# The first two column jobs of the in projection and of FFN up as plain products

## The chip, the cores and the metric

The kernel runs on one core of one Trainium2 chip. The time is device microseconds of one launch, and what is compared is the median of several runs. Engines are named as in the profile: PE is TensorE (matmuls and transposes), DVE VectorE, ACT ScalarE, POOL GpSimd, SP SyncE, which here only issues DMAs.

## The reference

One decoder layer, 1024 time steps of width 1024, float32 throughout:

```python
h = rmsnorm(x, norm_mix)
proj = h @ w_in                     # 1024 x N_IN; q, k, v, gates of three mixers
x = x + merged(gla, mlstm, fox) @ w_out
h = rmsnorm(x, norm_ffn)
u = causal_dwconv(h @ w_up, conv_w, conv_b)
a, g = jnp.split(u, 2, axis=-1)
x = x + (silu(g) * a) @ w_down
return rmsnorm(x, norm_final)
```

The two products that matter here are `h @ w_in`, and `h @ w_up` with its 5632 columns.

## The kernel before, in words

**Numbers.** A float32 product is made of three float32r matmuls: each operand is split into hi (a cast by ACT) and lo (source minus hi, by DVE) in `split` (L254), and the products hi x hi, hi x lo and lo x hi are added in PSUM (`prod`, L1135). One product of 512 by 512 by 512 is so 12 matmuls of 128x512. Operands live transposed: the moving side is a tile x of 128 features by 512 time steps.

**Jobs.** A `Job` (L45) makes two column tiles (m = 0, 1) of 128 columns over both time halves (hf = 0, 1) and both halves of the 1024 features (kh). That is eight block products; it needs seven, in the Winograd form of Strassen's scheme. They are numbered in the order 1, 5, 6, 2, 7, 3, 4. Each has a combination of the four weight blocks (`prep`, L1160, sums by POOL, then `wsplit`) and a combination of the four blocks of h. Call these b (the first half's eight blocks b0 to b7) and the second half's. x1 and x2 are blocks of the first time half; x3 is a block of the second; x5, x6, x7 and x4 are sums over both halves. The moving combinations are the same for all jobs of a stage. They are made once, put into the tiles g0 to g6 of the pool `big` (`put`, L344; `MAP_IN` and `MAP_FF` tell which) and stay for the whole stage.

**A stage's start.** The first four rows of 128 time steps are loaded, normalised and transposed (`blocks0`, L331), which gives x1 and x2; the second four follow (`blocks1`, L352), which makes x5, x6, x3, x7 and x4. `products` (L146) begins with the first two jobs, LEADS = 2, the leads: `rounds` (L182) takes them product by product, 1 for both, 2 for both, then 5, 6, 3, 7 and 4, so that work with x1 and x2 covers the making of the sums. From the third job on ("job 2", counted from 0) jobs run one after the other. `gemms` (L1233) prepares weights AHEAD = 2 products before they are used. In the in projection (`start`, L383) the leads are the gqk jobs of heads 0 and 1, job 2 is the first mx job. In the FFN the leads are the first two up jobs; their u tiles go through the convolution on DVE (L1316).

**Output.** The `post` functions (L1259, L1270) take a finished product out of PSUM: with a second operand by a DVE addition, without by an ACT copy; those of the in projection go through tiles st to DRAM by DMAs on SP. Near the end of the leads SP also loads wif and bt (L456, L464) for the small products pa<-wif,bt of the mLSTM gates, which PE computes between those of job 2.

**Order.** Each engine works off its own queue in order. The framework's scheduler places instructions of the whole program in those queues by its own estimates, so a change in the stage's start also shifts what stands next to what in the mixers. In the FFN's last stretch the finished activations come back as the down operand xd, whose splits use the tiles of `big` as they become free.

Of the kernel before, what the change touches and what calls it, by code (L numbers as in the profile page):

```python
# [35 lines left out]
MAP_IN = {1: 0, 2: 1, 5: 2, 6: 3, 3: 4, 7: 5, 4: 6}  # L36
MAP_FF = {1: 1, 2: 2, 5: 3, 6: 4, 3: 0, 7: 5, 4: 6}
# [4 lines left out]
KEEP = 14  # L42


class Job:  # L45
# [3 lines left out]
    def __init__(self, src1, src2, xc, post, name, nk=4, done=None, wide=False, kept=None):  # L49
        self.src, self.xc, self.post, self.name, self.nk = (src1, src2), xc, post, name, nk  # L50
        self.done, self.wide, self.kept = done, wide, kept
        self.raw, self.w, self.after = None, {}, {}
# [93 lines left out]
def products(jobs, lead=0, tail=0):  # L146


    yield from rounds(jobs[:lead])
# [24 lines left out]
def ending(jobs):  # L174

    yield from rounds(jobs, ROUND[:4])
    for j in jobs:
        for p in (7, 3, 4):
            yield j, p

# [8 lines left out]
class Kern:  # L189
# [162 lines left out]
    def blocks1(self, xs, b, pool, gain, xc, base, qtile, ttile):  # L352
        nc = self.nc
        t1, b22 = [], []
        for i in range(4):
            ps = self.turn4(xs, i)
            t = ttile(i)
            nc.vector.scalar_tensor_tensor(out=t, in0=ps, scalar=self.col(gain, i), in1=b[i],
                                           op0=ALU.mult, op1=ALU.subtract)
            t1.append(t)  # L360
            self.put(xc, 5, i, t, base)
        yield
        for i in range(4):
            ps = self.turn4(xs, 4 + i)
            q = qtile(i)
            nc.scalar.activation(q, ps, AF.Copy, scale=self.col(gain, 4 + i))
            b22.append(q)
            nc.vector.tensor_tensor(out=t1[i], in0=q, in1=t1[i], op=ALU.subtract)  # L368
            self.put(xc, 6, i, t1[i], base)
        yield  # L370
        for i in range(4):
            self.put(xc, 3, i, b22[i], base)
# [10 lines left out]
    def start(self, pool, xc, stream):  # L383
# [12 lines left out]
        xs = [self.norm(x, pool, i % 2) for i, x in enumerate(xs)]  # L396
        b = self.blocks0(xs, pool, "nm")
        xs = [load(tt) for tt in range(4, 8)]
        for i in range(4):
            self.put(xc, 1, i, b[i], MAP_IN)  # L400
        next(stream)
        next(stream)
        xs = [self.norm(x, pool, i % 2) for i, x in enumerate(xs)]
        for i in range(4):
            self.put(xc, 2, i, b[4 + i], MAP_IN, self.nc.gpsimd if i < 2 else None)
        for _ in range(2):
            next(stream)
        for _ in self.blocks1(xs, b, pool, "nm", xc, MAP_IN,
                                           lambda i: pool.tile([P, 512], F32, tag=f"q{i}", name=f"b22_{i}"),
                                           lambda i: pool.tile([P, 512], F32, tag="xs", name="t1", bufs=4)):  # L410
            for _ in range(2):
# [761 lines left out]

# [604 lines left out]
```

## Time and profile before

| | |
|---|---|
| runs | 2437.90, 2440.86, 2442.22 us; median 2440.86 us |
| profiled execution | 2440.24 us, span of its instructions 2438.4 us |
| PE | 2360.6 us busy, 97% of the span |
| DVE | 1599.3 us, 66% |
| ACT | 1145.9 us, 47% |
| POOL | 676.7 us, 28% |
| DMA | mean 130 GB/s |

The table's busy times are for the whole span. A stretch of the program is read from the busy time by stretch and from each engine's instructions in order of time. The lead stages are short: in the in projection from 20 us, in the FFN from 1748 us, each some 60 us.

### The profile page before, as it was taken

What the parts mean: (1) busy time and instruction counts of PE and PEld (TensorE: products, weight loads), DVE (VectorE), ACT (ScalarE), POOL (GpSimd) and SP (SyncE); (2) the same over time, 40 slices, a digit from 0 to 9 for tenths busy, and PEclk for the clock granted to TensorE, in tenths of its full rate; (3) what the DMA queues carried; (4) which work ended last, traced back from release to release, by engine and by line L of the source; (5) the groups of instructions that cost most, each with busy time, mean ns of one, the idle gap of its engine ahead of it and who ended that gap; (6) DMA issues with size and microseconds to landing.
All of it is one profiled execution on the core that took longest, in us unless ns stands there. A gap on an engine that the chain in (4) does not pass through costs nothing.

```text
span 2438.4 us, 32792 instructions
## 1 busy us (share of the span) xinstructions
PE 2360.6 (97%) x11359; PEld 1949.6 (80%) x11359; DVE 1599.3 (66%) x2871; ACT 1145.9 (47%) x2268; POOL 676.7 (28%) x752
## 2 busy tenths in 40 slices
PE   6999999989999999999999999999989999999998
PEld 4887778878888888888888888888868888888886
DVE  7697556767677775877776624534588998986223
ACT  5345455555566664555554512213355555554112
POOL 5222234444354443222222100000244443420000
PEclk9999999999999999999999999999999999999999
DMA  3355444545434444343343735421122222228232
GB/s 136 104 171 177 137 133 155 167 156 180 153 121 141 144 147 147 121 139 131 123 132 106 261 111 171 163 96 61 69 83 90 78 87 78 80 81 275 90 100 92
DMA packets 158500, 316.33 MB, mean 130 GB/s; under 512 B 16456, under 2 KB 56168, under 8 KB 157824
## 3 DMA queue, kind: packets, MB, share of 16 engines
q1 hardware_dynamic: 158336, 314.26, 39.0%
q8 instruction: 89, 1.46, 0.2%
q14 instruction: 75, 0.61, 0.1%
HBM read 218.61 MB, written 95.58 MB: 129 GB/s over the span
## 4 chain that ended last, share of the span: by engine, by line
PE 79%; DVE 8%; DMA 4%; ACT 3%; POOL 3%; issue 2%; SPq 0%; DVEq 0%; POOLq 0%; ACTq 0%
PE pg L248 49%; PE pa L248 28%; PE pa L252 3%; DMA mw<-mw_d 1%; DVE x L256 1%; POOL sum L1171 1%; POOL sm L261 1%; DVE w3l L256 0%; DVE st L1279 0%; DMA fv<-fv_d 0%; DMA fvo_raw<-in_w_in 0%; POOL mw L634 0%; DVE t L368 0%; DVE c L1316 0%; DVE e L805 0%
## 5 line engine op out<-in xcount | busy, mean ns | idle before, releaser
L248 PE MATMUL pg<-x,w6h 128*128 128x512 f32 x560 | 182.6, 404 | 11.8 <-DVE x L256 10.6
L248 PE MATMUL pg<-x,w4h 128*128 128x512 f32 x560 | 175.5, 394 | 1.3 <-DVE xm L1267 0.8
L248 PE MATMUL pg<-x,w1h 128*128 128x512 f32 x560 | 176.4, 395 | 0.0
L248 PE MATMUL pg<-x,w7h 128*128 128x512 f32 x560 | 175.2, 393 | 0.7 <-ACT u L1202 0.7
L248 PE MATMUL pg<-x,woh 128*128 128x512 f32 x512 | 158.1, 390 | 0.0
L248 PE MATMUL pa<-x,woh 128*128 128x512 f32 x512 | 157.7, 389 | 0.0
L1171 POOL TENSOR_TENSOR sum<-up_raw 128x512 f32<-128x512 f32 x44 | 87.5, 1989 | 227.1 <-DMA up_raw<-in_w_up 175.6
L1316 DVE SCALAR_TENSOR_TENSOR c<-u,cols,c 128x1022 f32<-128x1022 f32 x84 | 128.1, 1525 | 15.8 <-ACT c L1312 15.6
L248 PEld LDWEIGHTS pg<-x,w6h 128*128 128x128 f32 x560 | 106.1, 193 | 38.1 <-DVE x L256 14.1
L261 POOL TENSOR_TENSOR sm<-sm,mhalf 128x1 f32<-128x1 f32 (+1 forms) x32 | 27.9, 874 | 381.4 <-DVE sm L260 381.3
L248 PE MATMUL pg<-x,w2h 128*128 128x512 f32 x384 | 123.4, 398 | 1.6 <-POOL x L256 1.5
L248 PE MATMUL pg<-x,w5h 128*128 128x512 f32 x384 | 122.8, 398 | 0.9 <-DVE x L256 0.6
L248 PEld LDWEIGHTS pg<-x,w4h 128*128 128x128 f32 x560 | 103.7, 188 | 24.2 <-DVE xm L1267 1.2
L248 PE MATMUL pg<-x,w3h 128*128 128x512 f32 x384 | 123.0, 399 | 0.0
L248 PEld LDWEIGHTS pg<-x,w1h 128*128 128x128 f32 x560 | 103.8, 189 | 21.1 <-DVE x L256 0.5
L248 PEld LDWEIGHTS pg<-x,w7h 128*128 128x128 f32 x560 | 102.9, 188 | 22.0 <-ACT u L1202 1.2
L255 ACT CAST woh<-br_raw 128x512 fp32r<-128x512 f32 x48 | 29.9, 622 | 184.1 <-PE pa L248 177.4
L248 PE MATMUL pg<-x,w6l 128*128 128x512 f32 x280 | 112.9, 403 | 0.0
L248 PEld LDWEIGHTS pa<-x,woh 128*128 128x128 f32 x512 | 96.1, 188 | 20.0
L248 PEld LDWEIGHTS pg<-x,woh 128*128 128x128 f32 x512 | 96.1, 188 | 19.8
L248 PE MATMUL pg<-x,w1l 128*128 128x512 f32 x280 | 109.7, 392 | 0.0
L248 PE MATMUL pg<-x,w7l 128*128 128x512 f32 x280 | 109.4, 391 | 0.0
(459 smaller groups left out, 6748.1 us busy)
## 6 DMA issues: line engine op xcount, KB each, us to landing
up_raw<-in_w_up SPq DMA_DIRECT2D x44, 512.0 KB, 3.9
dn_raw<-in_w_dn SPq DMA_DIRECT2D x30, 512.0 KB, 4.0
gate_raw<-in_w_in SPq DMA_DIRECT2D x24, 512.0 KB, 3.7
g_d<-st SPq DMA_DIRECT2D x48, 256.0 KB, 2.4
yb<-y_d SPq DMA_DIRECT2D x48, 256.0 KB, 4.0
br_raw<-in_w_br SPq DMA_DIRECT2D x24, 512.0 KB, 4.6
gth<-g_d SPq DMA_DIRECT2D x48, 256.0 KB, 2.6
f_d<-c SPq DMA_DIRECT2D x22, 512.0 KB, 2.9
```

What stands on the lines that cost most here:

```text
L248: self.nc.tensor.matmul(out, lhsT=lhsT, rhs=rhs, start=start, stop=stop, skip_group_check=skip)
L252: self.nc.tensor.transpose(out=out, in_=in_, identity=self.ident[:k, :k])
L255: self.nc.scalar.copy(out=hi, in_=src)
L256: (eng or self.nc.vector).tensor_tensor(out=lo, in0=src, in1=hi.bitcast(F32), op=ALU.subtract)
L261: nc.gpsimd.tensor_tensor(out=out, in0=tmp, in1=self.mhalf[:, :n], op=ALU.pow)
L1171: self.nc.gpsimd.tensor_tensor(out=t, in0=a, in1=b, op=op)
L1316: nc.vector.scalar_tensor_tensor(out=c[:, s:], in0=u[:, :T - s], scalar=self.col("fw", 44 * tap + m), in1=c[:, s:], op0=ALU.mult, op1=ALU.add)
```

## The change

The leads of both stages are computed as plain products, eight quarters a job in place of seven products: `plain` gives their order, `quarter` computes one. A quarter's key is (hf, kh, m); its weights are a block as it is, without sums on POOL; two quarters add up in one PSUM bank, and ACT copies the result out. First come the eight quarters of the first time half, which need x1 and x2 alone, then eight of the second, which need x3 and a new x8, the other plain block of the second half; x8 lies in g6, where x4 later takes its place. `blocks1` makes x8 and x3 first (by ACT's scaled copy from PSUM), and then, in the program behind the quarters, x5 and x6 (subtractions by DVE) and x7 and x4 (by POOL). In the in projection the second four rows are loaded at once into the tile g5, ahead of the gqk weights, and x2 is split by DVE alone. In the FFN x3 and x7 change tiles, and the down operand takes the tiles in another order (`ROLL_DN`). `n` counts the two leads' products. The core of the diff:

```diff
-MAP_IN = {1: 0, 2: 1, 5: 2, 6: 3, 3: 4, 7: 5, 4: 6}
-MAP_FF = {1: 1, 2: 2, 5: 3, 6: 4, 3: 0, 7: 5, 4: 6}
+MAP_IN = {1: 0, 2: 1, 5: 2, 6: 3, 3: 4, 7: 5, 4: 6, 8: 6}
+MAP_FF = {1: 1, 2: 2, 5: 3, 6: 4, 3: 5, 7: 0, 4: 6, 8: 6}
+ROLL_DN = tuple(MAP_FF[p] for p in (1, 2, 5, 6, 7, 3, 4))
...
 def products(jobs, lead=0, tail=0):
-    yield from rounds(jobs[:lead])
+    yield from plain(jobs[:lead])
...
+def plain(jobs):
+
+    for kh in range(2):
+        for j in jobs:
+            for m in range(2):
+                yield j, (0, kh, m)
+    for j in jobs:
+        for kh in range(2):
+            for m in range(2):
+                yield j, (1, kh, m)
...
     def blocks1(self, xs, b, pool, gain, xc, base, qtile, ttile):
         nc = self.nc
         t1, b22 = [], []
+        for kh, tile, out, p in ((0, ttile, t1, 8), (1, qtile, b22, 3)):
+            for i in range(4):
+                ps = self.turn4(xs, 4 * kh + i)
+                t = tile(i)
+                nc.scalar.activation(t, ps, AF.Copy, scale=self.col(gain, 4 * kh + i))
+                out.append(t)
+                self.put(xc, p, i, t, base)
+            yield
         for i in range(4):
-            ps = self.turn4(xs, i)
-            t = ttile(i)
-            nc.vector.scalar_tensor_tensor(out=t, in0=ps, scalar=self.col(gain, i), in1=b[i],
-                                           op0=ALU.mult, op1=ALU.subtract)
-            t1.append(t)
-            self.put(xc, 5, i, t, base)
+            nc.vector.tensor_tensor(out=t1[i], in0=t1[i], in1=b[i], op=ALU.subtract)
+            self.put(xc, 5, i, t1[i], base)
         yield
         for i in range(4):
-            ps = self.turn4(xs, 4 + i)
-            q = qtile(i)
-            nc.scalar.activation(q, ps, AF.Copy, scale=self.col(gain, 4 + i))
-            b22.append(q)
-            nc.vector.tensor_tensor(out=t1[i], in0=q, in1=t1[i], op=ALU.subtract)
+            nc.vector.tensor_tensor(out=t1[i], in0=b22[i], in1=t1[i], op=ALU.subtract)
             self.put(xc, 6, i, t1[i], base)
-        yield
-        for i in range(4):
-            self.put(xc, 3, i, b22[i], base)
         yield
         for i in range(4):
             nc.gpsimd.tensor_tensor(out=b[i], in0=t1[i], in1=b[i], op=ALU.subtract)
...
         xs = [self.norm(x, pool, i % 2) for i, x in enumerate(xs)]
+        rows = self.group(MAP_IN[7], F32, "x")
+        later = [rows[:, i, :] for i in range(4)]
+        for i in range(4):
+            self.nc.sync.dma_start(out=later[i], in_=self.a["x"][(4 + i) * P:(5 + i) * P, :])
         b = self.blocks0(xs, pool, "nm")
-        xs = [load(tt) for tt in range(4, 8)]
         for i in range(4):
             self.put(xc, 1, i, b[i], MAP_IN)
-        next(stream)
-        next(stream)
-        xs = [self.norm(x, pool, i % 2) for i, x in enumerate(xs)]
+        for _ in range(2 * LEADS):
+            next(stream)
         for i in range(4):
-            self.put(xc, 2, i, b[4 + i], MAP_IN, self.nc.gpsimd if i < 2 else None)
-        for _ in range(2):
+            self.put(xc, 2, i, b[4 + i], MAP_IN)
+        xs = [self.norm(x, pool, i % 2) for i, x in enumerate(later)]
+        for _ in range(2 * LEADS):
             next(stream)
...
+            for _ in range((LEADS, 3 * LEADS)[n] if n < 2 else 0):
                 next(stream)
...
     def prep(self, job, p):
+        if isinstance(p, tuple):
+            _, kh, m = p
+            job.w[p] = self.wsplit(job.raw[2 * m + kh], "wp")
+            return
...
+    def quarter(self, job, hf, kh, m):
+
+        if kh == 0:
+            job.banks[hf, m] = self.pg()
+        bank = job.banks[hf, m]
+        wh, wl = job.w.pop((hf, kh, m))
+        x = job.xc[((1, 2), (8, 3))[hf][kh]]
+        for k in range(4):
+            ks = slice(k * P, (k + 1) * P)
+            xh, xl = x[k]
+            self.mm(bank, wh[:, ks], xh, kh == 0 and k == 0, False, True)
+            self.mm(bank, wh[:, ks], xl, False, False, True)
+            self.mm(bank, wl[:, ks], xh, False, kh == 1 and k == 3, True)
+        if kh:
+            job.post(m, hf, bank, None)
+            if hf and m and job.done is not None:
+                job.done()
...
-            n = 14
+            n = 16
...
-                    g = m // 2 % 7
+                    g = ROLL_DN[m // 2 % 7]
...
-            for _ in range(2 * LEADS):
+            for _ in range(4 * LEADS):
                 next(ff)
...
-                for _ in range(LEADS if n < 3 else 0):
+                for _ in range((LEADS, 3 * LEADS)[n] if n < 2 else 0):
                     next(ff)
```

SP's queue, at the program's start, before: names ending in a number are tiles, gqk_raw the weights of the leads, x_200 to x_206 the second four rows.

```order
L1155 DMA gqk_raw_217<-in_w_in 128x1024
L1155 DMA gqk_raw_219<-in_w_in 128x1024
L1155 DMA gqk_raw_225<-in_w_in 128x1024
L1155 DMA gqk_raw_227<-in_w_in 128x1024
L388 DMA x_200<-in_x 128x1024
L388 DMA x_202<-in_x 128x1024
L388 DMA x_204<-in_x 128x1024
L388 DMA x_206<-in_x 128x1024
```

And now, where x_144 is the tile of the second rows:

```order
L411 DMA x_144<-in_x 128x1024 x4
L1169 DMA gqk_raw_214<-in_w_in 128x1024
L1169 DMA gqk_raw_216<-in_w_in 128x1024
L1169 DMA gqk_raw_226<-in_w_in 128x1024
L1169 DMA gqk_raw_228<-in_w_in 128x1024
L1332 DMA gq_d_105<-st_347 128x512
```

The four row loads have moved from behind the gqk weights to ahead of them.

DVE's queue, in projection, before, where the last moving sums are split: x7 and x4 are tiles of moving sums, w7l and so on the lo parts of weights, st_535 an output tile.

```order
L256 TENSOR_TENSOR x7_560<-b0_149,x7_560 128x512
L256 TENSOR_TENSOR w7l_520<-sum3_517,w7h_519 128x512
L256 TENSOR_TENSOR x7_560<-b1_163,x7_560 128x512
L256 TENSOR_TENSOR w7l_541<-sum3_538,w7h_540 128x512
L1279 TENSOR_TENSOR st_535<-u2_486,pg_391 128x512
L256 TENSOR_TENSOR x7_560<-b2_177,x7_560 128x512
L256 TENSOR_TENSOR x7_560<-b3_191,x7_560 128x512
L256 TENSOR_TENSOR w4l_573<-gqk_raw_219,w4h_572 128x512
L256 TENSOR_TENSOR x4_611<-b4_156,x4_611 128x512
L1279 TENSOR_TENSOR st_556<-u2_506,pg_412 128x512
L256 TENSOR_TENSOR w4l_592<-gqk_raw_227,w4h_591 128x512
L256 TENSOR_TENSOR x4_611<-b5_170,x4_611 128x512
```

And now, from the last subtraction for x6 to the lo part of job 2's sixth weight sum:

```order
L382 TENSOR_TENSOR t1_440<-b22_3_511,t1_440 128x512
L269 TENSOR_TENSOR x7_658<-b0_154,x7_658 128x512
L269 TENSOR_TENSOR x7_658<-b1_168,x7_658 128x512
L269 TENSOR_TENSOR x6_645<-t1_440,x6_645 128x512
L269 TENSOR_TENSOR w5l_613<-sum1_610,w5h_612 128x512
L269 TENSOR_TENSOR x7_658<-b2_182,x7_658 128x512
L269 TENSOR_TENSOR x7_658<-b3_196,x7_658 128x512
L269 TENSOR_TENSOR x4_671<-b4_161,x4_671 128x512
L269 TENSOR_TENSOR x4_671<-b5_175,x4_671 128x512
L269 TENSOR_TENSOR x4_671<-b6_189,x4_671 128x512
L269 TENSOR_TENSOR x4_671<-b7_203,x4_671 128x512
L269 TENSOR_TENSOR w6l_719<-sum2_716,w6h_718 128x512
```

The weight splits and outputs of the leads, which stood between the splits of x7 and x4, are gone from there; w5l and w6l of job 2 stand among and behind these. From x8's first lo part to w6l the queue now has 39 operations.

ACT's queue, in projection, before, around the casts of x4: u2 are copies of a product for later use, st_643 an output tile.

```order
L255 CAST x4_611<-b4_156 128x512
L255 CAST x4_611<-b5_170 128x512
L255 CAST w4h_572<-gqk_raw_219 128x512
L255 CAST x4_611<-b6_184 128x512
L255 CAST x4_611<-b7_198 128x512
L255 CAST w4h_591<-gqk_raw_227 128x512
L255 CAST w1h_627<-mx_raw_623 128x512
L255 CAST w5h_648<-sum1_646 128x512
L255 CAST w6h_702<-sum2_700 128x512
L1283 COPY st_643<-pg_237 128x512
```

And now, where st_607 is the tile whose store stands on SP ahead of the loads of wif and of the first bt:

```order
L268 CAST x7_658<-b2_182 128x512
L268 CAST x6_645<-t1_440 128x512
L268 CAST w5h_612<-sum1_610 128x512
L268 CAST x7_658<-b3_196 128x512
L268 CAST x4_671<-b4_161 128x512
L268 CAST x4_671<-b5_175 128x512
L268 CAST x4_671<-b6_189 128x512
L268 CAST x4_671<-b7_203 128x512
L1322 COPY st_607<-pg_557 128x512
L268 CAST w6h_718<-sum2_716 128x512
```

The copy into st_607 stands behind the last cast of x4, whose source b7 is POOL's eighth subtraction. On PE, pa<-wif,bt moved from ahead of job 2's first product to the inside of its fifth. Near the FFN's end, the splits of the first four down operands now stand on DVE between the last weight splits of FFN up, where before they followed them.

## Rows read from the trace of the kernel before

**Rows 1.** The page: chain by engine, and the group of ACT's casts

```profile
PE 79%; DVE 8%; DMA 4%; ACT 3%; POOL 3%; issue 2%; SPq 0%; DVEq 0%; POOLq 0%; ACTq 0%
...
L255 ACT CAST woh<-br_raw 128x512 fp32r<-128x512 f32 x48 | 29.9, 622 | 184.1 <-PE pa L248 177.4
```

**Rows 2.** Busy time by stretch: length, then busy us of each engine (instructions), granted clock, DMA share

```profile
35.00:63.00 28.00, 19.14 (x81) 13.30 (x80) 27.95 (x25) 15.02 (x29) 21.27 (x13) 0.87 0.17 57
...
1759.00:1795.00 36.00, 25.91 (x102) 19.06 (x100) 29.98 (x33) 18.75 (x35) 21.02 (x13) 0.86 0.10 30
...
2145.00:2189.00 44.00, 44.00 (x195) 36.42 (x194) 35.65 (x40) 23.30 (x35) 10.76 (x7) 1.00 0.14 48
```

**Rows 3.** PE in order of time, in projection: start, us, engine, line, operation, count, [idle, releaser]

```profile
20.03 1.20 PE L248 MATMUL pg<-x,w1h 128*128 128x512 f32 x2
...
34.70 1.91 PE L252 MATMUL pa<-ident,x 128*128 128x128 f32 x16
...
51.09 0.80 PE L248 MATMUL pg<-x,w6h 128*128 128x512 f32 x1 [4.25 <-DVE x L256]
...
69.44 0.62 PE L248 MATMUL pg<-x,w7h 128*128 128x512 f32 x2
...
74.88 0.62 PE L248 MATMUL pg<-x,w4h 128*128 128x512 f32 x2
...
80.32 1.40 PE L248 MATMUL pa<-wif,bt 128*128 128x8 f32 x12
...
89.13 0.48 PE L248 MATMUL pg<-x,w6h 128*128 128x512 f32 x1
...
99.46 0.61 PE L248 MATMUL pg<-x,w1h 128*128 128x512 f32 x2
```

**Rows 4.** PE in order of time, the lead stage of FFN up

```profile
1747.63 0.62 PE L248 MATMUL pg<-x,w1h 128*128 128x512 f32 x2
...
1772.71 1.11 PE L252 MATMUL pa<-ident,x 128*128 128x128 f32 x4 [4.00 <-ACT b L366]
...
1806.72 0.62 PE L248 MATMUL pg<-x,w1h 128*128 128x512 f32 x2
...
1812.16 0.62 PE L248 MATMUL pg<-x,w6h 128*128 128x512 f32 x2
```

**Rows 5.** DVE in order of time, in projection

```profile
36.25 2.06 DVE L358 SCALAR_TENSOR_TENSOR t<-pa,cols,b 128x512 f32<-128x512 f32 x3
...
57.70 0.68 DVE L256 TENSOR_TENSOR w3l<-sum,w3h 128x512 fp32r<-128x512 f32 x1
58.30 1.77 DVE L256 TENSOR_TENSOR x<-b,x 128x512 fp32r<-128x512 f32 x1
60.00 1.75 DVE L256 TENSOR_TENSOR x<-t,x 128x512 fp32r<-128x512 f32 x1
...
78.28 1.82 DVE L256 TENSOR_TENSOR w6l<-sum,w6h 128x512 fp32r<-128x512 f32 x1 [1.59 <-ACT w6h L255]
```

**Rows 6.** DVE in order of time, FFN

```profile
1805.45 0.69 DVE L256 TENSOR_TENSOR w6l<-sum,w6h 128x512 fp32r<-128x512 f32 x1
...
1810.09 1.27 DVE L1316 SCALAR_TENSOR_TENSOR c<-u,cols,c 128x1023 f32<-128x1023 f32 x1
```

**Rows 7.** POOL in order of time, in projection

```profile
33.65 1.30 POOL L1171 TENSOR_TENSOR sum<-sum,gqk_raw 128x512 f32<-128x512 f32 x1 [0.33 <-POOL sm L261]
...
47.10 1.71 POOL L379 TENSOR_TENSOR b<-b,t 128x512 f32<-128x512 f32 x1
```

**Rows 8.** DMA, 0 to 60 us in 40 slices, then issues, 60 to 100 us (KB each, us to landing)

```profile
GB/s 0 205 251 281 369 398 424 407 421 276 38 0 0 35 265 396 371 325 5 0 0 0 5 173 78 109 0 0 0 0 87 268 0 0 0 0 0 60 281 8
...
wif<-in_wif SPq DMA_DIRECT2D x1, 96.0 KB, 4.3
```

**Rows 9.** DVE in order of time, the first splits of the down operand

```profile
2187.07 2.49 DVE L256 TENSOR_TENSOR xd<-dn_raw,xd 128x512 fp32r<-128x512 f32 x4
```

More of the change, by code (lines that the diff above doesn't have):

```diff
@@ L51, in __init__ @@
         self.done, self.wide, self.kept = done, wide, kept
-        self.raw, self.w, self.after = None, {}, {}
+        self.raw, self.w, self.after, self.banks = None, {}, {}, {}
         self.second, self.held, self.inplace, self.sum1 = False, None, False, None
@@ L396, in start @@
         xs = [self.norm(x, pool, i % 2) for i, x in enumerate(xs)]
+        rows = self.group(MAP_IN[7], F32, "x")
+        later = [rows[:, i, :] for i in range(4)]
+        for i in range(4):
+            self.nc.sync.dma_start(out=later[i], in_=self.a["x"][(4 + i) * P:(5 + i) * P, :])
         b = self.blocks0(xs, pool, "nm")
-        xs = [load(tt) for tt in range(4, 8)]
         for i in range(4):
             self.put(xc, 1, i, b[i], MAP_IN)
-        next(stream)
-        next(stream)
-        xs = [self.norm(x, pool, i % 2) for i, x in enumerate(xs)]
+        for _ in range(2 * LEADS):
+            next(stream)
         for i in range(4):
-            self.put(xc, 2, i, b[4 + i], MAP_IN, self.nc.gpsimd if i < 2 else None)
-        for _ in range(2):
+            self.put(xc, 2, i, b[4 + i], MAP_IN)
+        xs = [self.norm(x, pool, i % 2) for i, x in enumerate(later)]
+        for _ in range(2 * LEADS):
             next(stream)
-        for _ in self.blocks1(xs, b, pool, "nm", xc, MAP_IN,
+        for n, _ in enumerate(self.blocks1(xs, b, pool, "nm", xc, MAP_IN,
                                            lambda i: pool.tile([P, 512], F32, tag=f"q{i}", name=f"b22_{i}"),
-                                           lambda i: pool.tile([P, 512], F32, tag="xs", name="t1", bufs=4)):
-            for _ in range(2):
+                                           lambda i: pool.tile([P, 512], F32, tag="xs", name="t1", bufs=4))):
+            for _ in range((LEADS, 3 * LEADS)[n] if n < 2 else 0):
                 next(stream)
@@ L1192, in compute @@
         nc, post = self.nc, job.post
+        if isinstance(p, tuple):
+            self.quarter(job, *p)
+            return
         x = job.xc[p]
@@ L1536, in __call__ @@
             def __call__(self, j, m):
-                if m == 0 and j < LEADS:
-                    return lp.tile([P, T], F32, name=f"ua{j}")
+                if j < LEADS:
+                    return lp.tile([P, T], F32, name=f"u{m}{j}")
                 return self.pool.tile([P, T], F32, tag="u", name="u", bufs=4)
@@ L1620, in body @@
                 pass
-            for _ in range(2 * LEADS):
+            for _ in range(4 * LEADS):
                 next(ff)
             for n, _ in enumerate(k.blocks1([rows[tt] for tt in range(4, 8)], b, hp, "nf", xc, MAP_FF,
-                               lambda i: hp.tile([P, 512], F32, tag=f"q{i}", name="b22"),
+                               lambda i: hp.tile([P, 512], F32, name="b22") if i == 3 else
+                               k.swp.tile([P, 512], F32, tag="ws", name="b22", bufs=3),
                                lambda i: env["wide"].tile([P, 512], F32, tag="S", name="t1", bufs=4))):
-                for _ in range(LEADS if n < 3 else 0):
+                for _ in range((LEADS, 3 * LEADS)[n] if n < 2 else 0):
                     next(ff)
```

## Prediction

> **What bounds the kernel now.** The page's fifth section and its chain of waits come first: in the chain that ended last TensorE (PE) has 79% and VectorE (DVE) 8% [rows 1]. So time is won only where PE stands still or runs at its lower clock. The busy time by stretch says where that is: in 35 to 63 us PE works 19.14 of 28 us at a granted clock of 0.87, and in 1759 to 1795 us 25.91 of 36 us at 0.86; DVE is then busy for 27.95 and 29.98 us [rows 2]. These are the two lead stages, in the in projection and in FFN up. PE's order of time names what it waited for there: in projection a gap of 4.25 us that ended with a DVE write of x, and in the FFN one of 4.00 us that ended with a copy by ScalarE (ACT) [rows 3, 4]. They are the sums and hi/lo splits of the second four row blocks: the first half has too few products to cover them.
>
> The unit is read where nothing waits: the two w7 products of the leads, 24 matmuls, run from 69.44 to 74.88 us, 0.2267 us a matmul [rows 3], 2.72 us a product of 12. Sixteen transposes take 1.91 us [rows 3], a stage's 32 therefore 3.8 us.
>
> **What is removed and what is added.** Before, a stage's two leads are 14 products, 168 matmuls, 38.1 us, with transposes 41.9 us. They take from 20.03 to 80.32 us, where the next work (the small wif products) begins, and in the FFN from 1747.63 to 1806.72 us [rows 3, 4]: 60.3 and 59.1 us. So 18.4 and 17.2 us of wait and low clock can go. Added are two products per job, 48 matmuls in the two stages, 10.9 us of PE: a stage becomes 192 matmuls, 43.5 us, with transposes 47.3 us. If nothing else waited, the in projection would gain 13.0 and the FFN 11.8 us.
>
> The in projection also starts later. The second rows now stand on SyncE's (SP's) queue ahead of the four gqk weights, 2 MB; the stretch moved up to 424 GB/s [rows 8], so the weights can land up to 5 us later. The lower bound is nothing; I take 2.4, half, because the weights before were cast some us ahead of the first product. That leaves 10.6 us there, and 22.4 us with the FFN: a floor of 2417.8 us.
>
> **What is late next.** The sums have not gone; they are made during the second half, which PE runs through in eight products (21.8 us), the transposes, and job 2's products 1 and 5, before product 6 of job 2 needs x6 and w6l. DVE's queue shows, from the first lo part of x8 to w6l, 39 operations in a row, nearly all with two SBUF operands of 128x512. GpSimd (POOL) has 11 of that size beside them: three weight sums of job 2 and the eight subtractions for x7 and x4. An operation alone steps by 0.60 us (57.70 to 58.30); one that meets a POOL operation steps by 1.70 us (58.30 to 60.00), and POOL's then take 1.71 in place of 1.30 us [rows 5, 7]. So each POOL operation adds about 1.1 us to DVE. Bounds: over a whole stage of before, (29.98 - 33 x 0.60) / 13 = 0.8 us for each POOL operation in the FFN, and (27.95 - 25 x 0.60) / 13 = 1.0 us in the in projection [rows 2]. I take 1.1, as both queues are dense from x5 on. DVE then needs 39 x 0.60 + 11 x 1.1 = 35.5 us; at 0.8 it is 32.2.
>
> The row says 1.1 us for each. The Trainium skill, page "SBUF — State Buffer", section "Who interferes with whom", says that a DVE instruction with two SBUF inputs contends with a GpSimd instruction that reads SBUF, and that the second to issue fully blocks. By that, POOL's whole 1.30 us would be added, not 1.1: 2.2 us more in each stage. The trace shows the blocking, at a somewhat lower price.
>
> FFN: the first half's eight products end at 1747.63 + 96 x 0.2267 = 1769.4 us. A transpose, ACT's scaled copy and ACT's cast (0.62 us [rows 1]) lie before the first lo part; with waits for semaphores I take 2.8 us (the first sum of before starts 1.55 us after its transposes [rows 3, 5], without the cast). So DVE runs from 1772.2 to 1807.7 us. PE would be ready for product 6 at about 1801.4 (21.8 + 3.8 + 5.4 and a gap of 1), waits some 6 us, and starts it at about 1807.3, against 1812.16 [rows 4]: 4.9 us early. Behind w6l on DVE stand the convolutions of both leads, which before were partly worked off ahead of it: w6l began at 1805.45, and a tap takes 1.27 us [rows 6]. Six taps, 8 us, against the 5.4 us of products 6 and 2: 1 to 2 us are lost. Gain: 3.3 us (bounds: 0 and 9, the latter with DVE at 0.8 and the taps hidden).
>
> In projection: the first half ends at about 44.7, the first lo part of x8 starts at 47.4, w6l is written at 82.9 us; before, it began at 78.28 [rows 5]. POOL's last subtraction ends at about 76.5. Behind it, in ACT's queue, are the last cast of x4 and then the copy into st_607; behind its store on SP stand the loads of wif and the first bt. They go out at about 78.5 and land 4.3 us later [rows 8], near 82.8. The small product with wif now stands inside product 5 of job 2, so PE waits there, whatever DVE does. Product 6 follows at 86.2 to 87.8 us, against 89.13 [rows 3]. Two small groups that were done before it then are still to come (0.6 us each). Job 3's first product, 99.46 before [rows 3], comes 0.1 to 1.7 us earlier; I take 0.5, since a weight load is queued ahead of four later bt loads. Bounds: 4 us later (one more landing), 8 earlier (no wait for the store).
>
> Tail: the down operand's splits, 16 operations of 0.60 us (four took 2.49 [rows 9]), come in between the last two jobs' weight splits: 9.6 us, where DVE is idle 44 - 35.65 = 8.4 us before [rows 2]. PE has no gap there, and I charge 0.5 us (0 to 3); what DVE does earlier it need not do behind the last product, but PE does not wait for it there either. In the mixers the same work is placed one or two products differently. No row prices that; I leave it at 0, with 3 us to either side from its like, a gap of PE of up to 4.25 us [rows 3].
>
> Sum, against the profiled execution's 2440.24 us (1.84 around its span of 2438.4, 0.62 below the median): -0.5 - 3.3 + 0.5 = -3.3, so 2437 us.
>
> **The rivals.** *The chain is looser than I walked it.* POOL's operations meet DVE less often (0.8 us each), and st_607's copy comes through earlier. For it: the FFN's row of before is 0.8, and DVE has gaps there. Against: DVE's new queue is denser. In projection -4, FFN -6.5, tail +0.5: about 2430 us. Its end is the floor: all sums hidden, 2418.
>
> *The store in the in projection decides against the change.* ACT's copy into st_607 waits for POOL's eighth subtraction; from about 81 us on (instead of 78.5) for its issue, wif and bt land behind 85, a second landing (4.3 us) follows for the later bt behind the weight load, and PE's lower clock (after the 4.25 us gap of before the rows have a matmul at 0.8 us) adds 1 to 2. Job 3 then starts 6 to 9 us later than before; with the FFN's -3.3 and the tail's 0.5 that is 2443 to 2446 us, and 2450 where the FFN's taps are exposed too; I give it 2446. For it: three engines in series with no slack. Against: job 2's sums can be early, as its weights come once the first lead's last split is done.
>
> *The full block of the port* (the rule named above): 2.2 us more in each stage, 2441 us, within 0.2%.
>
> That the change doesn't do what it says I exclude: its queues show the eight plain products of each half in a row.
>
> **How the numbers follow.** The walked chain 0.36, the full block 0.08, the looser chain 0.30, nearly all hidden 0.08, the store 0.18. 0.2% is 4.9 us, about what a measurement of this kernel can tell from no change: the first two lie within it (0.44), the next two are faster (0.38), the last is slower (0.18). The range is 2426 to 2447 us: it takes in the looser chain with 3 us of the mixers' unknown and the store's value, and leaves out the floor and the store's far end.
>
> **What would show it.** Right: about 11 us more of PE matmul time in the two stages and no gap in the second half's eight products; then one gap of some 6 us ahead of product 6 in the FFN, ended by DVE's w6l, and one in the in projection inside product 5, ended by a DMA; DVE busy without a break from 47 to 83 and from 1772 to 1808 us. Wrong: w6l by 1803 (looser chain); gaps of PE in the first half, for the weights (a start later than 24 us); a job 3 that starts after 101 us (the store); gaps among the last products from 2145 to 2189 us, or a mixer stretch that changed by more than 3 us.

## The result, and the profile after

The changed kernel takes 2465.82 us (2463.44 to 2466.56), the kernel before 2439.38 us in the same comparison: a ratio of 1.0112, 95% interval 1.0099 to 1.0124. It is slower by some 26 us, where 2437 us and no measurable change were forecast, and the time lies outside the range. Its profiled execution has a span of 2464.0 us, 25.6 us more than the one before.

The page of after: busy time of the engines, and the engines of the chain. PE was busy for 2360.6 us before, 20.8 us less; 10.9 us of that are the 48 added matmuls (a product here is 512 features by 128 columns by 512 time steps, twelve matmuls). The rest goes with a lower clock: the mean granted clock over the span is 0.986, before 0.991. Answering to [rows 1], PE's share of the chain has fallen from 79 to 66%.

```profile
PE 2381.4 (97%) x11407; PEld 1966.6 (80%) x11407; DVE 1592.7 (65%) x2873; ACT 1155.0 (47%) x2288; POOL 655.4 (27%) x734
...
PE 66%; DVE 5%; ACT 2%; issue 2%; DMA 1%; POOL 1%; DVEq 0%; POOLq 0%; ACTq 0%; SPq 0%
```

Four marks on PE cut the span into pieces that can be compared: the first product of job 4 of the in projection, the first product of the FFN's leads, the first product of the last up job, and the first product with the down operand xd. (Job 4 is taken as the first mark, not job 3, because some of the small wif products stand behind job 3's first product in some of the kernels below.)

| stretch on PE, us | before | after | difference |
|---|---|---|---|
| start to job 4's first product | 120.46 | 129.23 | +8.8 |
| job 4 to the FFN's leads (mixers, output projection) | 1627.17 | 1638.27 | +11.1 |
| the FFN's leads to the last up job's w1 | 402.84 | 401.16 | -1.7 |
| last up job's w1 to the first xd | 38.08 | 44.43 | +6.4 |
| first xd to the end of the span | 249.85 | 250.91 | +1.1 |

Three of the pieces lose much, each far from its term of the sum; the FFN's piece alone is near to it. The rows that answer to [rows 3]: PE in order of time, in projection of after.

```profile
22.10 1.22 PE L261 MATMUL pg<-x,wph 128*128 128x512 f32 x2 [2.87 <-ACT wph L268]
...
45.69 2.84 PE L265 MATMUL pa<-ident,x 128*128 128x128 f32 x23
...
77.41 0.61 PE L261 MATMUL pg<-x,w1h 128*128 128x512 f32 x2
...
84.46 1.42 PE L261 MATMUL pa<-wif,bt 128*128 128x8 f32 x6 [3.94 <-DMA bt<-in_bdT]
...
92.98 1.20 PE L261 MATMUL pg<-x,w6h 128*128 128x512 f32 x2
...
100.38 0.52 PE L261 MATMUL pg<-x,w2l 128*128 128x512 f32 x1
...
108.24 0.62 PE L261 MATMUL pg<-x,w1h 128*128 128x512 f32 x2
```

The first product starts at 22.10 us, and the leads' sixteen products with their transposes end at 77.41, 2.9 us ahead of the 80.32 of [rows 3]. Then PE stands for 3.94 us inside job 2's product 5, until a bt tile lands, and the matmuls behind it take twice their time (two in 1.20 us at 92.98). Only from 100.38 us on are they fast again. The busy time by stretch, answering to [rows 2], gives the granted clock: 0.50 from 84 to 100 us, that is 1.2 in place of 2.4 GHz.

```profile
84.00:100.00 16.00, 15.54 (x49) 13.25 (x50) 4.88 (x13) 2.34 (x5) 2.60 (x3) 0.50 0.42 127
100.00:129.00 29.00, 29.00 (x147) 24.67 (x146) 17.91 (x25) 9.20 (x19) 8.33 (x5) 0.99 0.17 53
...
1816.00:1837.00 21.00, 16.49 (x64) 12.09 (x62) 21.00 (x20) 12.97 (x21) 12.34 (x7) 0.92 0.05 15
...
2168.66:2213.09 44.43, 41.14 (x170) 33.50 (x168) 39.26 (x50) 29.46 (x47) 13.68 (x7) 0.92 0.39 130
```

What bt waited for is on POOL, ACT and SP, in order of time: POOL's last subtraction; ACT's five casts of x7 and x4 and then the copy into st_607; SP's store from it, and behind it wif and bt.

```profile
77.44 1.75 POOL L390 TENSOR_TENSOR b<-b,t 128x512 f32<-128x512 f32 x1
```

```profile
77.51 2.71 ACT L268 CAST x<-b 128x512 fp32r<-128x512 f32 x5 [0.62 <-POOL b L386]
80.12 0.57 ACT L1322 COPY st<-pg 128x512 f32<-128x512 f32 x1
```

```profile
80.72 0.32 SPq L1332 DMA_DIRECT2D gq_d<-st  x1
81.13 0.38 SPq L470 DMA_DIRECT2D wif<-in_wif  x1
81.61 0.41 SPq L478 DMA_DIRECT2D bt<-in_bdT  x1
```

POOL's last subtraction ends at 79.2, the store goes out at 80.72, and bt is there at 84.4 us. DVE in order of time, answering to [rows 5, 6]: from x8's first lo part to w6l it has no break in the FFN, and in the in projection one of 2.37 us, for a cast by ACT.

```profile
48.47 1.29 DVE L269 TENSOR_TENSOR x<-t,x 128x512 fp32r<-128x512 f32 x2 [1.47 <-ACT x L268]
...
71.56 1.85 DVE L269 TENSOR_TENSOR x<-t,x 128x512 fp32r<-128x512 f32 x1 [2.37 <-ACT x L268]
73.33 1.78 DVE L269 TENSOR_TENSOR w1l<-mx_raw,w1h 128x512 fp32r<-128x512 f32 x1
...
84.94 0.68 DVE L269 TENSOR_TENSOR w6l<-sum,w6h 128x512 fp32r<-128x512 f32 x1
...
1792.04 1.29 DVE L269 TENSOR_TENSOR x<-t,x 128x512 fp32r<-128x512 f32 x2 [1.47 <-ACT x L268]
...
1828.20 0.68 DVE L269 TENSOR_TENSOR w6l<-sum,w6h 128x512 fp32r<-128x512 f32 x1
...
1829.40 2.47 DVE L1355 SCALAR_TENSOR_TENSOR c<-u,cols,c 128x1022 f32<-128x1022 f32 x2
```

That is 48.47 to 84.94, 36.5 us, and 1792.04 to 1828.20, 36.2 us, to the start of w6l. To its end, as the prediction counts the chain, it is 37.2 and 36.8 us, for 35.5 forecast. An operation that meets one of POOL takes 1.78 us, as in [rows 5]. On PE in the FFN, answering to [rows 4]:

```profile
1767.50 0.62 PE L261 MATMUL pg<-x,wph 128*128 128x512 f32 x2
...
1823.63 0.50 PE L261 MATMUL pa<-x,w5l 128*128 128x512 f32 x1 [3.75 <-DVE w5l L269]
...
1826.18 1.05 PE L261 MATMUL pa<-x,w5h 128*128 128x512 f32 x2
...
1828.28 0.73 PE L261 MATMUL pg<-x,w6h 128*128 128x512 f32 x2 [0.62 <-ACT s L1223]
...
1836.77 0.61 PE L261 MATMUL pg<-x,w1h 128*128 128x512 f32 x2
...
1858.02 0.62 PE L261 MATMUL pg<-x,w1h 128*128 128x512 f32 x2
```

Behind the gap of 3.75 us the matmuls take twice their time too (two in 1.05 us at 1826.18), but only until 1827.7 us.

### The profile page after: what moved, and what is told of

The parts are those of the page before. It is cut to its first block, busy times and chain, and to the rows that moved or that the text cites. A ratio compares the mean times of both kernels' runs of the same rounds, so it can differ in the third digit from the quotient of the medians.

```text
span 2464.0 us, 32922 instructions
## 1 busy us (share of the span) xinstructions
PE 2381.4 (97%) x11407; PEld 1966.6 (80%) x11407; DVE 1592.7 (65%) x2873; ACT 1155.0 (47%) x2288; POOL 655.4 (27%) x734
## 4 chain that ended last, share of the span: by engine, by line
PE 66%; DVE 5%; ACT 2%; issue 2%; DMA 1%; POOL 1%; DVEq 0%; POOLq 0%; ACTq 0%; SPq 0%
PE pg L261 40%; PE pa L261 23%; PE pa L265 3%; DVE c L1355 1%; DVE x L269 1%; DMA fv<-fv_d 1%; POOL sum L1185 0%; DVE e L819 0%; ACT L822 0%; DVE st L1318 0%; ACT L464 0%; DVE L L1059 0%; DVE L L1050 0%; DMA fvo_raw<-in_w_in 0%; DVE w5l L269 0%
## 5 line engine op out<-in xcount | busy, mean ns | idle before, releaser
L261 PE MATMUL pg<-x,w6h 128*128 128x512 f32 x528 | 169.4, 401 | 2.2 <-ACT s L1223 2.2
L261 PE MATMUL pg<-x,w7h 128*128 128x512 f32 x528 | 167.0, 397 | 3.3 <-ACT u L1223 3.3
L261 PE MATMUL pg<-x,w4h 128*128 128x512 f32 x528 | 167.2, 396 | 0.8 <-DVE xm L1306 0.8
L261 PE MATMUL pg<-x,w1h 128*128 128x512 f32 x528 | 166.5, 396 | 0.0
L1355 DVE SCALAR_TENSOR_TENSOR c<-u,cols,c 128x1022 f32<-128x1022 f32 (+1 forms) x88 | 134.6, 1535 | 14.1 <-ACT c L1351 14.0
L1185 POOL TENSOR_TENSOR sum<-up_raw 128x512 f32<-128x512 f32 x40 | 78.1, 1954 | 230.9 <-DMA up_raw<-in_w_up 175.1
L261 PE MATMUL pg<-x,w2h 128*128 128x512 f32 x368 | 116.7, 395 | 0.0
L269 DVE TENSOR_TENSOR fl<-f_raw,fh 128x512 fp32r<-128x512 f32 x44 | 30.3, 691 | 131.3 <-ACT fh L268 131.3
L261 PE MATMUL pa<-xd,fh 128*128 128x512 f32 x352 | 108.4, 389 | 0.0
L261 PE MATMUL pg<-xd,fh 128*128 128x512 f32 x352 | 108.3, 389 | 0.0
```

The costliest lines, as they stand in the source:

```text
L261: self.nc.tensor.matmul(out, lhsT=lhsT, rhs=rhs, start=start, stop=stop, skip_group_check=skip)
L269: (eng or self.nc.vector).tensor_tensor(out=lo, in0=src, in1=hi.bitcast(F32), op=ALU.subtract)
L1185: self.nc.gpsimd.tensor_tensor(out=t, in0=a, in1=b, op=op)
L1355: nc.vector.scalar_tensor_tensor(out=c[:, s:], in0=u[:, :T - s], scalar=self.col("fw", 44 * tap + m), in1=c[:, s:], op0=ALU.mult, op1=ALU.add)
```

## The experiments

Eleven more kernels ran. The marks are those of the table above; the number in brackets behind a time is the ratio to the kernel before in the same comparison (2437.3 to 2439.4 us) with its interval.

| kernel | us (ratio, interval) | to job 4 | mixers | FFN leads | to xd |
|---|---|---|---|---|---|
| before | 2439.4 | 120.5 | 1627.2 | 402.8 | 38.1 |
| after | 2465.8 (1.0112, 1.0099 to 1.0124) | 129.2 | 1638.3 | 401.2 | 44.4 |
| e1: after, n from 14 | 2453.7 (1.0063, 1.0047 to 1.0080) | 130.4 | 1623.8 | 401.2 | 43.4 |
| e2: the FFN's part alone | 2441.0 (1.0012, 1.0002 to 1.0021) | 122.0 | 1620.4 | 401.3 | 43.3 |
| e3: after, leads' stores on ACT | 2459.7 (1.0085, 1.0070 to 1.0100) | 124.9 | 1638.3 | 401.1 | 44.4 |
| e4: after, xd beginning with x3's tile | 2460.5 (1.0089, 1.0074 to 1.0104) | 131.7 | 1638.7 | 401.2 | 38.1 |
| e5: after, subtractions on DVE | 2445.4 (1.0029, 1.0020 to 1.0039) | 119.1 | 1639.3 | 395.9 | 43.3 |
| e7: before, n from 16 | 2451.1 (1.0056, 1.0038 to 1.0073) | 122.5 | 1636.2 | 402.9 | 38.1 |
| c1: e1, e3 and e4 together | 2439.5 (1.0012, 1.0001 to 1.0022) | 124.8 | 1621.8 | 401.1 | 38.1 |
| c4: all repairs | 2425.7 (0.9949, 0.9934 to 0.9964) | 114.0 | 1626.3 | 395.9 | 38.1 |
| e8: before, subtractions on DVE | 2420.8 (0.9927, 0.9911 to 0.9944) | 113.0 | 1626.1 | 391.8 | 38.1 |
| e9: e1, e4 and e5 together | 2429.9 (0.9965, 0.9952 to 0.9978) | 116.9 | 1626.2 | 396.1 | 38.1 |
| e10: c4, n from 12 | 2430.5 (0.9968, 0.9956 to 0.9979) | 113.0 | 1633.9 | 395.4 | 38.1 |

A difference between two kernels in one column needs a scale. Up to job 4 the code of after, e1 and e4 is the same as written, and they differ by 2.5 us; so is that of before, e2 and e7, and they differ by 2.0 us.

**Mixers: one number.** Theory: the count n decides at which products the loop takes an extra mixer step; with 16 it does so two products earlier than before. Rival: the in projection's lateness is carried on.

```diff
-            n = 16
+            n = 14
```

> The changed kernel with one number set back: n, the count from which the loop of the mixers decides where it takes an extra mixer step, starts at 14 instead of 16. From job 3's first product to the FFN's first one the changed kernel takes 1659.3 us (108.24 to 1767.50), the kernel before 1648.2 us (99.46 to 1747.63): 11.1 us more. Theory (phase): with 16 the extra steps fall two products earlier against the jobs than before, and the mixers' waits fall elsewhere; with 14 the stretch returns to 1648 to 1651 us and the run to about 2455 us. Rival (carried lateness: the in projection's late start and its weights shift the mixers' DMAs and engines whatever n is): the stretch stays at 1657 us or more and the run at about 2465 us.

The mixers took 1623.8 us with 14 and 1638.3 with 16, though the in projection was as late (from job 3, the stretch of the expectation: 1644.8 and 1659.3, a little more than was expected). The opposite edit, 16 in the kernel before:

> The kernel before with one number changed: n starts at 16 instead of 14, so the extra mixer steps fall two products earlier; nothing else of the change is in it. Theory (phase alone costs the mixers' stretch): from job 3's first product to the FFN's lead it takes 1655 to 1662 us instead of 1648.2, and the run 2446 to 2451 us. Rival (the phase costs only together with the plain leads): 1648 us and a run within 2 us of the kernel before.

1636.2 us (1657.2 from job 3), with nothing else of the change in it. And two products later:

```diff
-            n = 14
+            n = 12
```

> The kernel with all six repairs and n from 12, so that the extra mixer steps fall two products later than with 14. Theory (14 is a phase that the mixers' waits happen to fit, and a shift to either side costs): job 4 to the FFN's lead takes 1632 us or more instead of 1626.3 and the run is 2430 to 2440 us. Rival (only an earlier step costs, since the mixers then wait for their inputs): 1620 to 1627 us, the run at 2420 to 2427 us.

1633.9 us. Over all kernels, the seven with 14 have 1620.4 to 1627.2 us, the five with 16 have 1636.2 to 1639.3. The busy time by stretch, job 4 to the FFN's leads, after, then e1, has the loss as idle PE (39.6 against 32.1 us) and as slower matmuls (1598.71 against 1591.64 us for as many instructions):

```profile
129.23:1767.50 1638.27, 1598.71 (x7985) 1323.89 (x7983) 1032.79 (x2221) 792.07 (x1704) 441.74 (x601) 0.99 0.43 142
```

```profile
130.35:1754.12 1623.77, 1591.64 (x7985) 1319.17 (x7983) 1030.48 (x2221) 791.88 (x1704) 436.86 (x601) 1.00 0.44 143
```

The idle time is spread over many waits. PE's waits by releaser in after (total, times, longest) name two that stand in all five kernels with 16, with 2.8 and 2.2 to 2.3 us each time, and in none of the seven with 14:

```profile
PE pa L261 <- DVE att L879: 2.8, 1, 2.8
PE pa L265 <- DVE S L907: 2.2, 1, 2.2
```

Other waits grow and shrink beside them, and no run took apart why just these fit the one phase and not the other.

**Tail: the order of the tiles.** Theory: the down operand begins with a tile that is free early, so its splits get ahead of the last weight splits of FFN up, on ACT and on DVE. Rival: the gap comes from elsewhere.

```diff
-ROLL_DN = tuple(MAP_FF[p] for p in (1, 2, 5, 6, 7, 3, 4))
+ROLL_DN = (5, 1, 2, 3, 4, 0, 6)
```

> The changed kernel with the down operand's tiles taken in another order, beginning with the tile of x3, as in the kernel before, so that the first splits of xd wait for x3's last use. Theory (the splits of xd that got ahead of the last weight splits on ACT and DVE cost the tail): the gap of 3.29 us ahead of w7 at 2193.86 us and the low clock behind it go; from the last lead-like pair's w1 (2168.66) to the first product with xd it takes 38.1 us as before instead of 44.4; the run is about 2459 us. Rival (the tail's gap comes from the sum on POOL or from the weights, not from the splits): it stays, 2465 us.

The stretch went from 44.43 to 38.08 us, the time of before to the hundredth, and PE has no gap in it. So the place of the splits is the cause. The rows of after, in order of time, tell how. On DVE eight splits of xd stand ahead of w7l; POOL's sum for w3 waits for w7l and then takes 3.38 us beside DVE's next operations; on ACT w3h waits for that sum, and the copy u, for which PE waits, stands behind it:

```profile
2174.54 3.58 DVE L269 TENSOR_TENSOR xd<-dn_raw,xd 128x512 fp32r<-128x512 f32 x4
...
2183.35 2.49 DVE L269 TENSOR_TENSOR xd<-dn_raw,xd 128x512 fp32r<-128x512 f32 x4
...
2187.50 0.68 DVE L269 TENSOR_TENSOR w7l<-sum,w7h 128x512 fp32r<-128x512 f32 x1
```

```profile
2188.26 3.38 POOL L1185 TENSOR_TENSOR sum<-up_raw,sum 128x512 f32<-128x512 f32 x1 [7.17 <-DVE w7l L269]
```

```profile
2191.67 0.62 ACT L268 CAST w3h<-sum 128x512 fp32r<-128x512 f32 x1 [2.37 <-POOL sum L1185]
2192.20 1.13 ACT L268 CAST xd<-dn_raw 128x512 fp32r<-128x512 f32 x2
2193.24 0.58 ACT L1223 COPY u<-pg 128x512 f32<-128x512 f32 x1
```

```profile
2193.86 1.22 PE L261 MATMUL pg<-x,w7h 128*128 128x512 f32 x2 [3.29 <-ACT u L1223]
```

The same sum in the kernel before:

```profile
2167.53 1.29 POOL L1171 TENSOR_TENSOR sum<-up_raw,sum 128x512 f32<-128x512 f32 x1 [7.83 <-DVE w7l L256]
```

Counted from the last up job's first product, 2168.66 and 2150.47, the sum starts at 19.6 us in place of 17.1, 2.5 us later, and takes 2.1 us longer. That makes 4.6 us for w3h, and the copy u comes 4.7 us later. The two casts of xd on ACT between w3h and u add next to nothing: before, a copy and a cast of w4h stood there, which take as long.

**The FFN's part alone.** The in projection, its loads and n are those of before; of the FFN's part all is kept.

```diff
     yield from (first or plain)(jobs[:lead])
...
-            yield from products(ins, LEADS, TAIL)
+            yield from products(ins, LEADS, TAIL, rounds)
```

> Only the FFN's part of the change: the in projection's leads, its blocks1, its row loads and n = 14 are as before. Theory (three separate costs): in projection and mixers as before, the FFN's leads 1.7 us shorter, the tail 6 to 7 us longer, so about 2444 to 2446 us. Rival (the FFN's part is good by itself and the late tail comes from what the in projection left behind): 2436 to 2438 us.

2441.0 us: below the 2444 expected, and above the rival's 2438; the mixers came out at 1620.4 us in it, 6.7 us under before, for which no reason was found. The terms that the edit has are those of after: FFN's leads 401.3, tail 43.3 us. So the tail is the FFN part's own, and the rival, that the in projection left it behind, is out.

**In projection: the store.** Theory: PE waits for the store of st_607; rival: DVE's chain would hold it just as long.

```diff
-            nc.sync.dma_start(out=dst[:, sl], in_=t)
+            (nc.scalar if lead else nc.sync).dma_start(out=dst[:, sl], in_=t)
```

> The changed kernel, with the stores of the two lead jobs issued on ACT's queue instead of SP's, so that on SP the loads of wif and bt stand behind no store of the leads. Theory (the store is what PE waits for): PE's gap of 3.94 us inside product 5 of job 2 and the stretch at half clock behind it (84.5 to 100.4 us) go; w6l comes at about 85 us, product 6 starts there, and job 3's first product is at 98 to 100 us instead of 108.24; the run is about 2457 us if the mixers keep their length. Rival (DVE's chain alone is enough): the gap only moves to product 6, PE falls to half clock all the same, and job 3 starts at 104 us or later.

Neither came out whole: job 3 started at 103.88 us, between the two. The gap of 3.94 us became one of 1.32 us for w5l (so DVE's chain does hold PE, by that much), and a second one came up at the third small product, which waits for a bt tile: there are two of these, and the load of the third goes out only when PE has used the first. PE fell to half clock behind that gap too.

```profile
81.27 0.50 PE L261 MATMUL pg<-x,w5l 128*128 128x512 f32 x1 [1.32 <-DVE w5l L269]
...
88.80 1.14 PE L261 MATMUL pa<-wif,bt 128*128 128x8 f32 x6 [2.26 <-DMA bt<-in_bdT]
...
92.92 1.05 PE L261 MATMUL pg<-x,w6h 128*128 128x512 f32 x2
```

**DVE and POOL.** Theory: each POOL operation of 128x512 holds DVE up by 1.1 us, more than the 0.60 us that the same operation costs on DVE. Rival: POOL's work was mostly hidden.

```diff
-            nc.gpsimd.tensor_tensor(out=b[i], in0=t1[i], in1=b[i], op=ALU.subtract)
+            nc.vector.tensor_tensor(out=b[i], in0=t1[i], in1=b[i], op=ALU.subtract)
...
-            nc.gpsimd.tensor_tensor(out=b[4 + i], in0=b[4 + i], in1=t1[i], op=ALU.subtract)
+            nc.vector.tensor_tensor(out=b[4 + i], in0=b[4 + i], in1=t1[i], op=ALU.subtract)
```

> The changed kernel with the eight subtractions for x7 and x4 on DVE instead of POOL, in both stages. Theory (each POOL operation holds DVE up by about 1.1 us): from x8's first lo part to w6l it takes 36.5 us in the in projection (48.47 to 85) and 36.2 us in the FFN (1792.0 to 1828.2); with eight operations of 0.60 us more on DVE and eight of 1.1 us of hold-up less it is 32 to 33 us in both. PE's gap of 3.75 us ahead of w5l in the FFN shrinks to 1 us or less, the FFN's leads gain 3 to 4 us, the in projection 2 to 4 (ACT's copy into st_607 no longer waits for POOL), the run is 2458 to 2462 us. Rival (POOL's work was mostly hidden): the chain grows by 4 to 5 us to about 41 us and the run to 2468 us or more.

DVE in order of time, both stages:

```profile
51.31 1.29 DVE L269 TENSOR_TENSOR x<-t,x 128x512 fp32r<-128x512 f32 x2 [1.47 <-ACT x L268]
...
83.60 0.69 DVE L269 TENSOR_TENSOR w6l<-sum,w6h 128x512 fp32r<-128x512 f32 x1
...
1782.95 1.29 DVE L269 TENSOR_TENSOR x<-t,x 128x512 fp32r<-128x512 f32 x2 [1.47 <-ACT x L268]
...
1815.20 0.68 DVE L269 TENSOR_TENSOR w6l<-sum,w6h 128x512 fp32r<-128x512 f32 x1
```

51.31 to 83.60 is 32.3 us, and 1782.95 to 1815.20 is 32.25: 4 us less, with eight operations more. So the eight on POOL had cost 4 + 8 x 0.60 = 8.8 us, 1.1 us each. In the in projection 2.37 us of this were the wait for ACT's cast, which is gone here; without it the price there is 0.8 us. By the Trainium skill's full block ("SBUF — State Buffer", "Who interferes with whom") each would cost POOL's whole 1.30 us [rows 7], an estimate of 10.4 us in all. The runs bear out that POOL holds DVE up, and the price per operation is below that. That need not mean a weaker block: beside each other DVE steps by 1.70 us and POOL takes 1.71 [rows 5, 7], which would be POOL's 1.30 and 0.4 of DVE's own 0.60, in turn. No run tested this reading.

The run came out 20 us below after, not 4 to 8. (Its profiled execution was the slowest of its ten; its pieces in the table account for 16.5.) The FFN's leads gave 5.2, a little more than the theory has it. The in projection gave 10.1: ACT's copy into st_607 no longer waits for POOL, PE's longest gap from job 2 on to the first small product is 0.67 us, and the granted clock stays at 1.00 through the same small products:

```profile
74.00:95.00 21.00, 20.33 (x101) 16.77 (x100) 15.73 (x29) 10.58 (x19) 6.62 (x7) 1.00 0.38 123
```

So the small products by themselves do not lower the clock; in after a gap of 3.94 us stood ahead of them.

**Together.** The three repairs of e1, e3 and e4:

> The changed kernel with three repairs at once: n from 14, the down operand's tiles beginning with x3's, and the leads' stores on ACT's queue. Theory (three separate costs, which add): 11 to 14.6 us less in the mixers, 6.3 less in the tail, 4.4 less ahead of job 3: 2441 to 2444 us. Rival (they share a cause): less than 15 us in all, 2450 us or more.

2439.5 us, a little better than expected: the costs add (by the ratios 12, 6.6 and 5.6 us apart, 24.4 us together), and the kernel is back at about the time of before, which it does not beat. Then the subtractions on DVE, a third bt tile, and the second rows loaded behind the weights:

```diff
-        for i in range(4):
-            self.nc.sync.dma_start(out=later[i], in_=self.a["x"][(4 + i) * P:(5 + i) * P, :])
...
-        for _ in range(2 * LEADS):
+        next(stream)
+        for i in range(4):
+            self.nc.sync.dma_start(out=later[i], in_=self.a["x"][(4 + i) * P:(5 + i) * P, :])
+        for _ in range(2 * LEADS - 1):
             next(stream)
...
-            bt = mp.tile([P, 3, P], F32, tag="bt", name="bt", bufs=2)
+            bt = mp.tile([P, 3, P], F32, tag="bt", name="bt", bufs=3)
```

> The same three repairs, and three more: the eight subtractions on DVE, the second four rows loaded behind the gqk weights, and three bt tiles instead of two. Theory: the first product at 20 us instead of 22.1; the DVE chain some 4 us shorter in both stages; no gap of PE inside product 5; job 3's first product at 96 to 99 us; the FFN's leads 4 to 5 us shorter than in the kernel before; the run at 2430 to 2436 us, under the kernel before. Rival (what bounds the stage's start is the small products' loads, whatever DVE does): job 3 at 101 us or later, the run at 2438 us or more.

2425.7 us, better than expected: 15.2 us less than after up to job 4, and 6.9 us less than before in the FFN's leads. Without the third tile, the rows' move and the stores' move:

> The changed kernel with n from 14, the down operand's tiles beginning with x3's, and the eight subtractions on DVE; the leads' stores stay on SP's queue, there are two bt tiles, and the second rows are loaded ahead of the weights. Theory (with the subtractions on DVE the copy into st_607 no longer waits for POOL, so nothing else is needed against the gap inside product 5): job 4's first product at 117 to 120 us, the run at 2428 to 2432 us. Rival (the store on SP still holds wif and bt back): a gap of 2 us or more ahead of a small product, job 4 at 124 us or later, 2434 us or more.

2429.9 us, 116.9 us to job 4: the store on SP costs no more than a few us once ACT's copy does not wait for POOL.

**Without the plain products.** The last question is what the plain leads give by themselves. The kernel before, with the eight subtractions on DVE and nothing else (the edit of e5):

> The kernel before, with only the eight subtractions for x7 and x4 on DVE instead of POOL, in both stages. It asks how much of the gain of the repaired version belongs to that and not to the plain leads. Theory (the hold-up of DVE by POOL costs the leads' seven-product form as well): DVE's chain is some 4 us shorter in each stage, the in projection and the FFN's leads gain 2 to 4 us each, the run is 2430 to 2434 us. Rival (in the seven-product form POOL's weight sums hold DVE up anyway, and the subtractions stand in the way of the leads' weight splits): within 2 us of the kernel before, about 2438 us.

2420.8 us, 17 us under before and some 10 us better than expected, and the lowest time of all; the intervals of its ratio and of c4's overlap a little. So two lines of the kernel before do at least as much as the whole change with all its repairs. The busy time by stretch shows where: POOL does less, DVE's operations are 37 in place of 25 in the same 28 us, and PE works for 23.85 us in place of 19.14 at a granted clock of 1.00 in place of 0.87 [rows 2].

```profile
35.00:63.00 28.00, 23.85 (x113) 17.66 (x111) 27.90 (x37) 17.07 (x31) 11.95 (x7) 1.00 0.21 66
...
1750.00:1787.00 37.00, 32.35 (x150) 24.73 (x149) 36.40 (x52) 24.20 (x41) 13.91 (x6) 1.00 0.18 54
```

```profile
47.24 0.50 PE L248 MATMUL pg<-x,w6h 128*128 128x512 f32 x1 [1.02 <-DVE x L256]
...
73.64 0.39 PE L248 MATMUL pg<-x,w4l 128*128 128x512 f32 x1
```

PE's gap of 4.25 us of [rows 3] is 1.02 us. The leads' fourteen products are done at 74.0 us, behind the last w4l, against 77.41 us for the sixteen of after, and in the FFN the stretch is 391.8 us against 395.9 us for plain leads with the same subtractions on DVE. In the FFN's leads alone e8 gains 11.0 us, where 2 to 4 were expected. Of the 19.5 us by which its span is shorter than before, 10.0 are PE's busy time, with as many matmuls, and 9.5 its idle time: where the gaps went, the low clock behind them went too.

## Why the prediction was wrong

**Right: the limits and the chain.** The first product started at 22.10 us (20.03 + 2.4 forecast), the first half ended at 45.7 (44.7 forecast; the terms give 44.2), and the chain of sums on DVE took 37.2 and 36.8 us (35.5 forecast). The price for each POOL operation came out at 0.8 to 1.1 us, within the bounds of the forecast. In the in projection PE's gap stood inside product 5 and was ended by a DMA, as forecast. In the FFN it was forecast ahead of product 6, with some 6 us, for w6l; 3.75 us came inside product 5, for w5l, and 0.62 us ahead of product 6, for a copy by ACT. FFN's product 6 came 60.8 us after the leads' start against 64.5 before, 3.8 us early (4.9 forecast). Job 3 was 4.5 us early, and 2.8 us of that were lost again in it and in the next job (21.25 and 19.60 us in place of 19.04), where 1 to 2 us were walked for the taps; that it was the taps, which stand behind w6l on DVE, fits the rows but was not tried. The sum there, -1.7 for -3.3, has the right sign and half the size.

One sign of being right failed without harm: the second half's eight products had gaps. In the in projection they were 0.63 to 0.88 us long, each ended by a lo part from DVE, and with low clock behind them that half took 31.7 us in place of 25.6; job 2 waited for the DMA all the same.

**Wrong, in the in projection: the term of -0.5 was +8.8.** The step that failed is "Product 6 follows at 86.2 to 87.8 us". The wait came as walked: bt landed at 84.4, where 82.8 was forecast; POOL's last subtraction had ended 2.7 us later than walked. What the step left out is what follows a gap. From 84.46 to 100.38 us PE ran at half clock, and product 6 began at 92.98. The rival of the store named this, with 1 to 2 us for the clock, and its 6 to 9 us for job 3 held (+8.8); it was given 0.18 and, for the whole, at most 2450 us.

**Wrong, in the mixers: the term of 0, with 3 us to either side, was +11.1.** The step that failed took the mixers' order as scatter without a price. n was read as a count of the leads' products. But the loop tests n against a threshold and a period, so the extra steps moved by two products, all in one direction: e1 and e7 show 14.5 and 9.0 us for the shift by itself, in either kernel, and e10 7.6 us for a shift to the other side: of the three values run, 14 is the best. The bound of 3 us came from the length of one gap; what was at stake was all of PE's idle time there, 33.2 us before and 39.6 after, and its clock, 4.8 us more for the same matmuls.

**Wrong, in the tail: 0.5 (0 to 3) was +6.4.** The step counted DVE's operations against its idle time over the stretch, and from there being no gap of PE before took it that there would be none. It left out the order: the splits of xd stood ahead of w7l, POOL's sum waited for w7l and then ran beside DVE for 3.38 us in place of 1.29, and w3h and the copy u on ACT waited behind it. The step walked neither POOL's queue nor ACT's. PE's gap of 3.29 us took another 3 us of lower clock with it (0.92 over the stretch). That the splits' place costs the 6.4 us is shown by e4; the way from DVE over POOL to ACT is read from the rows, and no run moved the splits of one engine alone.

**Missing from the rivals.** None asked what bounds the leads in the kernel before. Its DVE was busy for 27.95 of 28 us there [rows 2], with 1.1 us for a POOL operation in it [rows 5]: the same row that priced the new chain also said that POOL's subtractions were a cost of the old one. e8 shows that this was the nearer remedy.

## What to carry to other kernels

Where VectorE is the limit and GpSimd works on the same memory, an operation moved to GpSimd is not free: here it cost VectorE 0.8 to 1.1 us to save 0.60. A count that starts a periodic order is part of the schedule, and whoever changes it moves everything behind it. When work moves, walk every queue that it enters, and those that wait for it, for instructions that now stand in front of others, and price the clock behind a gap of TensorE as well as the gap.

## What was not expected of the hardware

The cost of a gap on TensorE was not its length. In after, the gap of 3.94 us in the in projection was followed by 16 us at a granted clock of 0.50, with four groups of small products in them; behind the gap of 3.75 us ahead of w5l in the FFN, with none, the matmuls were slow until 1827.7 us and at full speed from 1828.28 us on. In the kernel before, the gap of 4.25 us [rows 3] stood in a stretch of 28 us at 0.87 [rows 2].

Nor does a low clock need a long gap. In e2, PE in order of time, a gap of 0.65 us ahead of a small product is all there is, and the granted clock from 86.50 to 90.20 us is 0.54:

```profile
84.39 0.83 PE L261 MATMUL pa<-wif,bt 128*128 128x8 f32 x6 [0.65 <-DMA bt<-in_bdT]
...
87.57 1.06 PE L261 MATMUL pg<-x,w5h 128*128 128x512 f32 x2
```

In e5 the small products behind a gap of 0.67 us ran at 1.00. So the small products may have a part in the low clock, and in how long it lasted in after; no run moved them alone, and what tells these cases apart stays open.
